# A hybrid decoder step on one core: x of three SSD groups turned to tokens by VectorE and DRAM instead of TensorE

## The chip, the core and the metric

The kernel runs on one core of a Trainium2 chip. The time is device microseconds from the first to the last instruction of an execution, with what lies around them; a few executions are taken of each kernel, and one more is recorded by the hardware profiler. Engines are named as the profile does: PE (TensorE), DVE (VectorE), ACT (ScalarE), POOL (GpSimd) and SP (SyncE), which mostly issues DMAs.

## The reference

One decoder layer is computed for 320 tokens: 256 of a prompt and 64 samples (8 sequences of 8 new tokens). `proj = rms_norm(x) @ w_in` gives the columns of a gated chunk MLP and of an SSD mixer; both results go through `w_out`, and a convolutional FFN follows. Of the mixer, the change touches the part that works on x:

```python
xbc, new_conv = causal_depthwise_conv(xbc, conv_state, conv_w, conv_b)
xbc = jax.nn.silu(xbc)
xs = xbc[..., :SSM_WIDTH].reshape(bsz, L, SSM_HEADS, SSM_HEAD_DIM)
...
xdt = (x * dt[..., None]).reshape(bsz, nc, q, G, R, P)
...
y_diag = jnp.einsum("bctsgr,bcsgrp->bctgrp", cb[..., None] * decay, xdt)
...
states = jnp.einsum("bcsgn,bcsgr,bcsgrp->bcgrpn", bc, decay_states, xdt)
```

There are 4 groups (G) of 8 heads of 64 columns. A group's x is 512 columns of `proj` by 320 tokens, and each token's x is multiplied by a step width dt per head.

## The kernel before

**Projections.** All matrix products keep the tokens in the free dimension: a weight slab of 128 x 1024 numbers is loaded by SP into `wraw` (L117), ACT rounds it to `whi` (L123), DVE takes the rest to `wlo` (L124), each with three buffers, and PE makes three products of 128 x 320 per weight block: `whi` with the high and the low part of the activations and `wlo` with the high part (L134 to L136), 24 products per slab. `project` makes columns of w_in, four blocks of 128 in four buffers of PSUM (`ps_0` to `ps_3`), `chunk_out` a part of w_out, whose sums `pd` DVE adds to `acc_mix` (L247). DVE also evacuates the projections (`ev`, L390).

**Background tasks.** Behind each slab, `tick` lets a task go one step further. `ssd(g)` is such a task, one for each group 0 to 3, called first to fourth group here. It begins with the preparation (x to tokens, xdt, cb, x0s), then `s_ps` with the products around it, and then steps n = 0 to 12 (11 in the last group), in which the states are updated, decays are made on ACT, DVE and POOL, and the outputs are multiplied. The order on each engine is that in which the program writes the instructions, but for priorities (`first`) and explicit positions (`issue_after`). `heads_in_next(g)` projects the group's x and appends the task; around the change the sequence is: heads_in of g + 1, w_out part, heads_out (z) of g. So the last steps of a group run under the w_out part, and the next group's preparation follows under its end and the start of z.

**x of a group.** `conv_proj` leaves `xs` (128 columns, 4 blocks, 320 tokens) after the last Silu (L460). At the group's start PE turns it by products with the identity: `by_token` (L412) eight times 128 x 128 for the 256 tokens of the prompt, into `xt_ps`, and DVE multiplies by dt (`times`, L925) to `xdt`. POOL multiplies the first half by a decay (`decayed`, L930, x0d), ACT and DVE split that into the parts of `x0s` (L981, L982), which `s_ps` (L991) multiplies. `x_of_samples` (L937) turns the 64 samples in four products behind `s_ps`; `samples_split` (L925, L946) and `samples_rows` (L956) multiply these. At the end of a group POOL multiplies the state `s` (L1140), and SP stores it and a second tile (L1148, L1149), to be loaded for the end of the mixer (L1160, L1161).

**B.** For the columns of B the kernel has a way without PE: `to_tokens` lets DVE turn 32 x 32 blocks (L418), for 64 tokens of four blocks at a time, POOL's queue writes them to a DRAM tile with DMAs of 32 tokens x 2 x 128 columns (L420), and loads bring rows of tokens back (L839). The 32 x 32 blocks leave the columns in an order of their own, which `in_order` undoes.

**The start.** x itself arrives in pieces by ACT's queue (`load_x`, L602): pieces of 1, 1, 2 and 2 blocks of 320 columns at first, and then two more whenever an even block has been split, six blocks ahead.

## Time and profile before

| what | us |
|---|---|
| median of 3 runs (lowest, highest) | 1748.01 (1747.86, 1748.75) |
| the profiled execution | 1748.47 |
| its span, first to last instruction | 1746.8 |
| PE busy, share of the span | 1738.5, 100% |
| DVE, ACT, POOL busy | 1178.0, 819.4, 323.5 |

Times in the trace count from the first instruction. A row of the timeline gives start, duration, engine, line, operation and operands (out<-in, shapes, count of instructions grouped), and in brackets idle time before it with what ended it. Products are pipelined: one lasts longer than the distance to the next, so PE's time is read from start to start. A "DMA to landing" row gives the least, median and greatest time from the issue of the DMAs of one line to the arrival of their data.

### The profile page before, as it was taken

Reading aid. Unit: us, or ns where it says so; the run is one execution under the profiler, and the core shown is the slowest. Engines: PE = TensorE matmul, PEld = TensorE weight load, DVE = VectorE, ACT = ScalarE, POOL = GpSimd, SP = SyncE. Lnnn points to the kernel's source line nnn. Section 1 sums busy time; section 2 is a strip of 40 time slices with the busy share of each in tenths; the row PEclk is TensorE's granted clock in tenths of the full one; section 3 lists DMA queues with packets and bytes.
Section 4 is the critical chain, followed back from the end, with each engine's and each line's share of the span. In section 5 each row is a group of like instructions: output and inputs, shape, how many; then the busy total and the mean of one; then the engine's idle time right before and its main releaser. Section 6 shows DMA issues by size and latency. Waiting matters only on the chain.

```text
span 1746.8 us, 31126 instructions
## 1 busy us (share of the span) xinstructions
PE 1738.5 (100%) x12063; PEld 1719.3 (98%) x12063; DVE 1178.0 (67%) x2009; ACT 819.4 (47%) x1198; POOL 323.5 (19%) x684
## 2 busy tenths in 40 slices
PE   9999999999999999999999999999999999999998
PEld 9999999999999999999999999999999999999997
DVE  6549863657879787778954566565756565657587
ACT  6344545334656664646544434343434343333336
POOL 2432230000423323121210101020201010101002
PEclk9999999999999999999999999999999999999999
DMA  8786655456676777665655554545544545454543
GB/s 257 230 231 183 183 176 154 151 163 192 214 221 208 218 225 210 211 187 155 195 154 151 151 154 149 150 155 147 159 145 151 155 149 152 152 153 151 148 158 109
DMA packets 228803, 303.85 MB, mean 174 GB/s; under 512 B 21680, under 2 KB 152624, under 8 KB 228464
## 3 DMA queue, kind: packets, MB, share of 16 engines
q1 hardware_dynamic: 211264, 272.68, 51.7%
q0 software_dynamic: 6176, 13.87, 2.7%
q10 hardware_dynamic: 11216, 15.31, 2.6%
q8 instruction: 95, 1.56, 0.4%
q14 instruction: 52, 0.43, 0.1%
HBM read 280.80 MB, written 19.69 MB: 172 GB/s over the span
## 4 chain that ended last, share of the span: by engine, by line
PE 99%; DMA 0%; ACT 0%; DVE 0%; SPq 0%; issue 0%; ACTq 0%
PE ps L134 21%; PE ps L135 20%; PE ps L136 20%; PE pd L134 10%; PE pd L135 10%; PE pd L136 10%; PE y_ps L1086 1%; PE ps_v L134 1%; PE ps_v L136 1%; PE ps_v L135 1%; PE yo_ps L1001 0%; PE up_ps L1018 0%; PE sg L808 0%; DMA wraw<-in_w_in 0%; PE fin_ps L1167 0%; PE xt_ps L412 0%
## 5 line engine op out<-in xcount | busy, mean ns | idle before, releaser
L124 DVE TENSOR_TENSOR wlo<-wraw,whi 128x1024 fp32r<-128x1024 f32 (+2 forms) x480 | 584.7, 1219 | 420.6 <-ACT whi L123 417.8
L123 ACT CAST whi<-wraw 128x1024 fp32r<-128x1024 f32 (+2 forms) x479 | 495.4, 1034 | 693.4 <-PE ps L135 392.3
L134 PE MATMUL ps<-h_hi,whi 128*128 128x320 f32 x2428 | 752.2, 310 | 0.0
L135 PE MATMUL ps<-h_lo,whi 128*128 128x320 f32 x2428 | 750.6, 309 | 0.0
L136 PE MATMUL ps<-h_hi,wlo 128*128 128x320 f32 x2428 | 750.0, 309 | 0.0
L134 PEld LDWEIGHTS ps<-h_hi,whi 128*128 128x128 f32 x2428 | 455.7, 188 | 3.1 <-issue 1.3
L135 PEld LDWEIGHTS ps<-h_lo,whi 128*128 128x128 f32 x2428 | 455.9, 188 | 0.4
L136 PEld LDWEIGHTS ps<-h_hi,wlo 128*128 128x128 f32 x2428 | 455.7, 188 | 0.0
L134 PE MATMUL pd<-fhi,whi 128*128 128x320 f32 x704 | 217.4, 309 | 0.0
L135 PE MATMUL pd<-flo,whi 128*128 128x320 f32 x704 | 217.4, 309 | 0.0
L136 PE MATMUL pd<-fhi,wlo 128*128 128x320 f32 x704 | 217.4, 309 | 0.0
L134 PE MATMUL pd<-ohi,whi 128*128 128x320 f32 x448 | 138.7, 310 | 0.0
L136 PE MATMUL pd<-ohi,wlo 128*128 128x320 f32 x448 | 138.3, 309 | 0.0
L135 PE MATMUL pd<-olo,whi 128*128 128x320 f32 x448 | 138.3, 309 | 0.0
L1341 POOL COPY ptf<-pad 128x2 f32<-128x2 f32 x88 | 22.0, 250 | 601.4 <-DVE pad L1329 600.8
L136 PEld LDWEIGHTS pd<-fhi,wlo 128*128 128x128 f32 x704 | 132.4, 188 | 0.0
L134 PEld LDWEIGHTS pd<-fhi,whi 128*128 128x128 f32 x704 | 132.3, 188 | 0.0
L135 PEld LDWEIGHTS pd<-flo,whi 128*128 128x128 f32 x704 | 132.3, 188 | 0.0
L247 DVE TENSOR_TENSOR acc_ffn<-acc_ffn,pd 128x320 f32<-128x320 f32 (+1 forms) x161 | 77.2, 480 | 29.8 <-PE pd L136 28.2
L134 PEld LDWEIGHTS pd<-ohi,whi 128*128 128x128 f32 x448 | 84.1, 188 | 0.6
L135 PEld LDWEIGHTS pd<-olo,whi 128*128 128x128 f32 x448 | 84.1, 188 | 0.3
L136 PEld LDWEIGHTS pd<-ohi,wlo 128*128 128x128 f32 x448 | 84.1, 188 | 0.0
(353 smaller groups left out, 1725.0 us busy)
## 6 DMA issues: line engine op xcount, KB each, us to landing
wraw<-in_ffn_w_up SPq DMA_DIRECT2D x176, 512.0 KB, 3.7
wraw<-in_w_in SPq DMA_DIRECT2D x132, 512.0 KB, 3.8
wraw<-in_ffn_w_down SPq DMA_DIRECT2D x88, 512.0 KB, 3.4
wraw<-in_w_out SPq DMA_DIRECT2D x64, 512.0 KB, 3.5
st<-in_state_ssm SPq DMA_DIRECT2D x40, 256.0 KB, 4.6
out_ssm_state_sample<-st ACTq DMA_DIRECT2D x30, 256.0 KB, 2.3
cs<-dacs_d SPq DMA_DIRECT2D x16, 320.0 KB, 5.3
wraw<-in_w_in SPq DMA_DIRECT2D x12, 384.0 KB, 3.8
```

The source lines that it names most:

```text
L123: rounded[:] = [act.copy(hi, raw).ins]
L124: lowered[:] = [dve.tensor_tensor(out=lo, in0=raw, in1=hi.bitcast(F32), op=ALU.subtract).ins]
L134: pe.matmul(ps, whi, xhi, start=first, stop=False)
L135: pe.matmul(ps, whi, xlo, start=False, stop=False)
L136: last_made[0] = pe.matmul(ps, wlo, xhi, start=False, stop=last).ins
L247: added_last[:] = [dve.tensor_tensor(out=acc[:, nb, ts], in0=acc[:, nb, ts], in1=ps[:, ts], op=ALU.add).ins]
L1086: pe.matmul(ps[64 * i:64 * i + 64, cols], w(hl), x(hl, m, cpx), tile_position=(0, 64 * i), **flags)
L1341: pool.tensor_copy(ptf[:, k, :], pad[:, 256:258])
```

## The change

For groups 1 to 3 the turning by PE goes. In steps 7, 8 and 9 of the preceding group DVE turns the 320 tokens of `xs` in five pieces of 64 (two, two, one), and POOL's queue writes each piece with two DMAs to a DRAM tile `x_d`. In step 11 two loads on POOL's queue bring the 256 prompt tokens back as `x_raw` (tag `xsp`), and at the group's start a third brings the samples as `x_raw_s`, in the tile of the tag `s1`, which `s` of the preceding group also uses. `times_raw` multiplies by dt, two instructions where there was one, for the order of the columns. `samples_rows` stands before the step, not in n == 0. The first group keeps PE's way. B's writes, which share the code, become ten DMAs of 4 x 32 x 128 in place of twenty of 32 x 2 x 128. At the start, the piece of x of blocks 4 and 5 is no longer loaded with the first, and later pieces are loaded four blocks ahead.

```diff
--- before.py
+++ after.py
@@ -356,6 +356,7 @@
     tot_d = dr.tile([NH, NB], F32, name="tot_d")
     s1_d, x1_d = ([dr.tile([P, 512], F32, name=f"{n}_d{g}") for g in range(3)] for n in ("s1", "x1"))
     b_d = dr.tile([NT, 512], F32, name="b_d")
+    x_d = [dr.tile([NT, 512], F32, name=f"x_d{g}") for g in range(1, 4)]
     v_d = [dr.tile([NT, 2 * P], F32, name=f"v_d{i}") for i in range(KD // 2)]
     ssq_d = [dr.tile([P, NT // 32], F32, name=f"ssq_d{i}") for i in range(4)]
@@ -411,13 +412,17 @@
         pe.transpose(ps, x[:, P * c:P * c + P], ident)
+    def tokens_at(x, rows, o):
+
+        t = tp.tile([P, NT], F32, tag="pv", name="turned", bufs=4)[:, :4 * NS].rearrange("p (r f) -> p r f", r=2)
+        dve.transpose(out=t.rearrange("p r (j f) -> p r j f", j=4), in_=x[:, :, o:o + NS].rearrange("p j (r t) -> p r j t", t=32))
+        for r in range(2):
+            pool.dma_start(rows[o + 32 * r:o + 32 * r + 32].rearrange("t (i f) -> i t f", i=4), t[:, r])
+
     def to_tokens(x, rows):
         for o in range(0, NT, NS):
-            t = tp.tile([P, NT], F32, tag="pv", name="turned", bufs=4)[:, :4 * NS].rearrange("p (r f) -> p r f", r=2)
-            dve.transpose(out=t.rearrange("p r (j f) -> p r j f", j=4), in_=x[:, :, o:o + NS].rearrange("p j (r t) -> p r j t", t=32))
-            for i in range(4):
-                pool.dma_start(rows[o:o + NS, P * i:P * i + P].rearrange("(r t) f -> t r f", t=32), t[32 * i:32 * i + 32])
+            tokens_at(x, rows, o)
             yield
     def in_order(ap):
@@ -601,7 +606,7 @@
                 cs = slice(KD + NT * k if k else 0, KD + NT * (k + n))
                 act.dma_start(flat[:, cs], xT[:, cs])
             with tc.high_priority(offset=300000):
-                for k, n in ((0, 1), (1, 1), (2, 2), (4, 2)):
+                for k, n in ((0, 1), (1, 1), (2, 2)):
                     load_x(k, n)
                     if k == 1:
                         act.activation(held, ones[:, 0:1], AF.Square)
@@ -616,9 +621,9 @@
                         x_split.append(act.activation(hT[0][:, kt, :], x, AF.Copy, scale=pre[:, kt:kt + 1]).ins)
                         x_low.append(dve.scalar_tensor_tensor(out=hT[1][:, kt, :], in0=x, scalar=pre[:, kt:kt + 1],
                                                               in1=hT[0][:, kt, :].bitcast(F32), op0=ALU.mult, op1=ALU.subtract).ins)
-                        if kt % 2 == 0 and kt < 10:
+                        if kt % 2 == 0 and kt < 12:
                             with tc.issue_after(x_split[-1]):
-                                load_x(kt + 6, 2)
+                                load_x(kt + 4, 2)
             def x_squares(kt):
@@ -896,7 +901,7 @@
                 return ap.rearrange("p (h d) -> p h d", d=64)
             x_of = {0: x0}
-            rest, y_made, b_later = [], {}, []
+            rest, y_made, b_later, raw_of = [], {}, [], {}
             def ssd(g):
@@ -925,6 +930,15 @@
                     dve.tensor_tensor(out=by_head(out), in0=by_head(ps),
                                       in1=dt[at, c, h0 + h.start:h0 + h.stop].unsqueeze(2).to_broadcast([at.stop - at.start, n, 64]), op=ALU.mult)
+                def times_raw(out, raw, c, at=slice(0, P), js=slice(0, 4)):
+
+                    n = raw.shape[0]
+                    for h in range(2):
+                        o = out.rearrange("p (j h i f) -> p h j i f", j=4, h=2, f=32)[:, h, js]
+                        d = dt[at, c, h0:h0 + 8].rearrange("p (j h) -> p h j", h=2)[:, h, js]
+                        dve.tensor_tensor(out=o, in0=raw[:, 256 * h:256 * h + 256].rearrange("p (i j f) -> p j i f", j=4, f=32)[:, js],
+                                          in1=d.unsqueeze(2).unsqueeze(3).to_broadcast([n, js.stop - js.start, 2, 32]), op=ALU.mult)
+
                 def decayed(i, c):
                     xde = sd.tile([P, 512], F32, tag="xde", name="xde", bufs=2)
                     pool.tensor_tensor(out=by_head(xde), in0=by_head(xdt[:, c, :]),
@@ -939,7 +953,10 @@
                 def samples_split(ps):
                     xq = sd.tile([P, 512], F32, tag="xde", name="xq", bufs=2)
-                    times(xq[:NS], ps[:NS], 3, slice(0, NS))
+                    if g:
+                        times_raw(xq[:NS], ps, 3, slice(0, NS))
+                    else:
+                        times(xq[:NS], ps[:NS], 3, slice(0, NS))
                     for i in range(2):
                         o = slice(32 * i, 32 * i + 32)
                         act.copy(xsp[o, i], xq[o])
@@ -953,16 +970,26 @@
                 def samples_rows(ps):
                     for r in range(2):
                         at, hs = slice(NS - NS * r, P - NS * r), slice(256 * r, 256 * r + 256)
+                        if g:
+                            times_raw(xdt[at, 2, :], ps, 2, slice(0, NS), slice(2 * r, 2 * r + 2))
+                            continue
                         dve.tensor_tensor(out=by_head(xdt[at, 2, hs]), in0=by_head(ps[:NS, hs]),
                                           in1=dt[:NS, 2, h0 + 4 * r:h0 + 4 * r + 4].unsqueeze(2).to_broadcast([NS, 4, 64]), op=ALU.mult)
                 for c in range(2):
-                    ps = misc("xt_ps")
-                    for j in range(4):
-                        by_token(ps[:, P * j:P * j + P], xs[:, j], c)
-                    times(xdt[:, c, :], ps, c)
+                    if g:
+                        times_raw(xdt[:, c, :], raw_of[g][0][:, c], c)
+                    else:
+                        ps = misc("xt_ps")
+                        for j in range(4):
+                            by_token(ps[:, P * j:P * j + P], xs[:, j], c)
+                        times(xdt[:, c, :], ps, c)
                     if c == 0:
                         x0d = decayed(0, 0)
+                if g:
+                    raw = sd.tile([P, 512], F32, tag="s1", name="x_raw_s", bufs=1)
+                    pool.dma_start(raw[:NS], x_d[g - 1][NP:NT])
+                    raw_of[g].append(raw)
                 ps = misc("cb_ps")
                 for c in range(2):
                     pe.matmul(ps[:, P * c:P * c + P], bT[:, g, P * c:P * c + P], cT[:, g, P * c:P * c + P],
@@ -989,7 +1016,7 @@
                 ps_s = misc("s1_ps")
                 for i, (b, x) in enumerate(((0, 0), (0, 1), (1, 0))):
                     pe.matmul(ps_s, btok[:, b, bs], x0s[:, x], start=i == 0, stop=i == 2)
-                ps_x = x_of_samples()
+                ps_x = raw_of[g][1][:NS] if g else x_of_samples()
                 ps_yo = misc("yo_ps")
@@ -1041,8 +1068,9 @@
                 for i in range(4):
                     with_c(i, sts[i] if i < 3 else st3)
                 xsp = sd.tile([P, 2, 512], F32R, tag="xsp", name="xsp", bufs=1)
+                samples_split(ps_x)
+                samples_rows(ps_x)
                 s1 = sd.tile([P, 512], F32, tag="s1", name="s1", bufs=1)
-                samples_split(ps_x)
                 act.copy(s1, ps_s)
                 strips(0)
                 yield 24, 0
@@ -1105,7 +1133,6 @@
                 decays_of = {0: (1, 2), 7 - e: (3,)}
                 for n in range(13 - e):
                     if n == 0:
-                        samples_rows(ps_x)
                         yo_to_xdt()
                     if n in ends and not (n == 10 and g == 3):
                         end(ends[n])
@@ -1125,7 +1152,15 @@
                         b_raw = sd.tile([P, 512], F32, tag="st", name="b_later", bufs=6)
                         sp.dma_start(b_raw, b_d[P:2 * P])
                         b_later.append(b_raw)
+                    if n in (7, 8, 9) and g < 3:
+                        with tc.issue_after(lowered[0]):
+                            for o in ((0, 1), (2, 3), (4,))[n - 7]:
+                                tokens_at(x_of[g + 1], x_d[g], NS * o)
                     if n == 11 and g < 3:
+                        raw = sd.tile([P, 2, 512], F32, tag="xsp", name="x_raw", bufs=1)
+                        for c in range(2):
+                            pool.dma_start(raw[:, c], x_d[g][P * c:P * c + P])
+                        raw_of[g + 1] = [raw]
                         with tc.issue_after(lowered[0]):
                             mask_c(g + 1)
                     if n in shrinks:
```

On PE, the start of the fourth group (in the order, `x8` counts instructions of one kind; `pd_13` and `pd_14` are sums of w_out, `ps_3` is the fourth block of z). Before:

```order
L136 MATMUL pd_13_7629<-ohi,wlo 128x320
L412 MATMUL xt_ps<-ident,xs 128x128 x8
L968 MATMUL cb_ps<-cT,bT 128x128 x2
L971 MATMUL cb_ps<-cT,bT 64x64 x2
...
L136 MATMUL ps_3_7713<-h_hi,wlo 128x320
L991 MATMUL s_ps<-x0s,btok 128x512 x3
L937 MATMUL xt_ps<-ident,xs 64x128 x4
L1001 MATMUL yo_ps<-st,cb_cms 32x256 x12
```

Now:

```order
L136 MATMUL pd_13_7675<-ohi,wlo 128x320
L995 MATMUL cb_ps<-cT,bT 128x128 x2
L998 MATMUL cb_ps<-cT,bT 64x64 x2
...
L136 MATMUL ps_3_7753<-h_hi,wlo 128x320
L1018 MATMUL s_ps<-x0s,btok 128x512 x3
L1028 MATMUL yo_ps<-st,cb_cms 32x256 x12
```

The eight products ahead of `cb_ps` and the four behind `s_ps` have gone; the rest of the order stays.

On POOL, from the last writes of the third group to the first work of the fourth. Before:

```order
L1140 TENSOR_TENSOR s_6732<-s_6732,dec 128x512
L1063 TENSOR_TENSOR cpx<-cpx,cT 128x256
L930 TENSOR_TENSOR xde<-xdt,dec 128x512
L1012 TENSOR_TENSOR st<-st,tote 128x512 x6
L930 TENSOR_TENSOR xde<-xdt,dec 128x512
L1063 TENSOR_TENSOR cpx<-cpx,cT 128x256
```

Now:

```order
L420 DMA x_d_108<-turned 4x32x128 x10
L1162 DMA x_raw<-x_d_108 128x512
L1175 TENSOR_TENSOR s_6763<-s_6763,dec 128x512
L1162 DMA x_raw<-x_d_108 128x512
L1091 TENSOR_TENSOR cpx<-cpx,cT 128x256
L991 DMA x_raw_s<-x_d_108 64x512
L944 TENSOR_TENSOR xde<-xdt,dec 128x512 x2
L1039 TENSOR_TENSOR st<-st,tote 128x512 x6
L1091 TENSOR_TENSOR cpx<-cpx,cT 128x256
```

Ten writes and three loads have come between, and `xde` of the fourth group, before right behind the third's last work, now stands behind the load of the samples.

On DVE, around the addition of `pd_14` and up to `x0s` of the fourth group. Before:

```order
L247 TENSOR_TENSOR acc_mix<-acc_mix,pd_13_7629 128x320
L925 TENSOR_TENSOR xdt<-xt_ps,dt 128x512
L124 TENSOR_TENSOR wlo<-wraw,whi 128x1024
L925 TENSOR_TENSOR xdt<-xt_ps,dt 128x512
L973 TENSOR_TENSOR cb_cms<-cb_ps,upper 128x256
L247 TENSOR_TENSOR acc_mix<-acc_mix,pd_14_7681 128x320
L976 TENSOR_TENSOR cb_cms<-cb_ps,upper_s 64x64
L977 TENSOR_TENSOR cb_cms<-cb_ps,upper_s 64x64
L982 TENSOR_TENSOR x0s<-xde,x0s 128x512
```

Now:

```order
L1000 TENSOR_TENSOR cb_cms<-cb_ps,upper 128x256
L124 TENSOR_TENSOR wlo<-wraw,whi 128x1024
L939 TENSOR_TENSOR xdt<-x_raw,dt 128x4x64
L247 TENSOR_TENSOR acc_mix<-acc_mix,pd_14_7721 128x320
L939 TENSOR_TENSOR xdt<-x_raw,dt 128x4x64
L1003 TENSOR_TENSOR cb_cms<-cb_ps,upper_s 64x64
L939 TENSOR_TENSOR xdt<-x_raw,dt 128x4x64 x2
L1004 TENSOR_TENSOR cb_cms<-cb_ps,upper_s 64x64
L247 TENSOR_TENSOR acc_mix<-acc_mix,pd_15_7735 128x320
L1103 TENSOR_TENSOR cs<-cs,cb_cms 128x320
L124 TENSOR_TENSOR wlo<-wraw,whi 128x1024
L1009 TENSOR_TENSOR x0s<-xde,x0s 128x512
```

The multiplications by dt are split and mixed with other work, an addition, a `cs` and a `wlo` now stand ahead of `x0s`. The turnings stand some rows earlier:

```order
L247 TENSOR_TENSOR acc_mix<-acc_mix,pd_10_7600 128x320
L418 STREAM_TRANSPOSE turned<-xs 128x256 x3
L247 TENSOR_TENSOR acc_mix<-acc_mix,pd_11_7614 128x320
L418 STREAM_TRANSPOSE turned<-xs 128x256
L124 TENSOR_TENSOR wlo<-wraw,whi 128x1024
L887 TENSOR_TENSOR cb_cms<-cmask,cT 128x128 x2
L1125 SCALAR_TENSOR_TENSOR xs<-xs,prm,y_ps 128x320
```

Three of the five are ahead of the addition of `pd_11`, the fourth behind it; the fifth follows two rows on.

## The prediction

> **What bounds the kernel now.** I read the page first: span, busy shares, granted clock, the chain that ended last.
>
> ```profile
> span 1746.8 us, 31126 instructions
> ...
> PE 1738.5 (100%) x12063; PEld 1719.3 (98%) x12063; DVE 1178.0 (67%) x2009; ACT 819.4 (47%) x1198; POOL 323.5 (19%) x684
> ...
> PEclk9999999999999999999999999999999999999999
> ```
> ```profile
> PE 99%; DMA 0%; ACT 0%; DVE 0%; SPq 0%; issue 0%; ACTq 0%
> ```
>
> PE is the chain, at full granted clock in every slice. Next, the list of what PE waited for (in all, times, longest), then the busy times of PE, PEld, DVE, ACT and POOL in the 40 us around the start of the fourth group:
>
> ```profile
> PE early L69 <- DVE ones L65: 1.1, 1, 1.1
> PE both L1454 <- ACT f_tok L1452: 1.0, 1, 1.0
> PE ps_v L134 <- ACT whi L123: 0.5, 1, 0.5
> ```
> ```profile
> 660.00:700.00 40.00, 40.00 (x314) 38.13 (x313) 29.45 (x44) 19.64 (x35) 14.78 (x11) 1.00 0.72 216
> ```
>
> Three waits, 2.6 us in all, two at the start and one in the tail: around the change PE never waits. So a matmul removed there is time saved in full, and every new wait of PE is time lost in full. The question is whether x by the new way is there as early as x by PE was.
>
> **What is removed.** PE's timeline at the start of the fourth group, where one row may hold several instructions of a kind:
>
> ```profile
> 670.01 1.03 PE L412 MATMUL xt_ps<-ident,xs 128*128 128x128 f32 x8
> 670.88 0.61 PE L968 MATMUL cb_ps<-cT,bT 128*128 128x128 f32 x4
> ```
> ```profile
> 678.86 0.85 PE L991 MATMUL s_ps<-x0s,btok 128*128 128x512 f32 x3
> 679.55 0.60 PE L937 MATMUL xt_ps<-ident,xs 128*64 128x128 f32 x4
> 680.08 1.93 PE L1001 MATMUL yo_ps<-st,cb_cms 128*32 128x256 f32 x32
> ```
>
> From start to next start the eight turnings take 670.88 − 670.01 = 0.87 us, 0.109 each. Four of the samples at that pitch are 0.44; by the start behind them 680.08 − 679.55 = 0.53, which holds a change of operand that stays. I take 0.87 + 0.44 = 1.31, at most 1.40. Three groups: **−3.92** (at most −4.2).
>
> **What DVE is given.** The five turnings per group are the operation that the trace shows for B (three in 1.09), and each multiplication of a whole x (0.69, below) becomes two halves.
>
> ```profile
> 239.14 1.09 DVE L418 STREAM_TRANSPOSE turned<-bT 128x256 f32<-128x256 f32 x3
> ```
>
> That is some 5 × 0.36 = 1.8 us, and small change for more instructions, spread over steps in which DVE is busy 29.45 of 40 us and hands wlo over before PE asks for it (PE's list of waits has no wlo). I cost it at nothing; bounds 0 and, if wlo came late by all of one step's three turnings, 1.1.
>
> **What the fourth group's x now needs.** The rows of x before: ACT's last Silu of xs, then DVE, POOL and ACT from the turned x to x0s, on which s_ps (678.86) waits:
>
> ```profile
> L460 ACT ACTIVATE xs<-cv x16: 239/243/254, 208.1 to 662.6; 128x64 f32<-128x64 f32 x16
> ```
> ```profile
> 662.97 1.23 DVE L124 TENSOR_TENSOR wlo<-wraw,whi 128x1024 fp32r<-128x1024 f32 x1
> 664.11 0.49 DVE L247 TENSOR_TENSOR acc_mix<-acc_mix,pd 128x320 f32<-128x320 f32 x1
> ```
> ```profile
> 670.65 0.69 DVE L925 TENSOR_TENSOR xdt<-xt_ps,dt 128x512 f32<-128x512 f32 x1
> ...
> 674.69 0.67 DVE L982 TENSOR_TENSOR x0s<-xde,x0s 128x512 fp32r<-128x512 f32 x1
> 675.29 0.48 DVE L1075 TENSOR_TENSOR cs<-cs,cb_cms 128x320 f32<-128x320 f32 x1
> ...
> 676.49 1.21 DVE L124 TENSOR_TENSOR wlo<-wraw,whi 128x1024 fp32r<-128x1024 f32 x1
> ```
> ```profile
> 666.44 1.88 POOL L1140 TENSOR_TENSOR s<-s,dec 128x512 f32<-128x512 f32 x1 [18.64 <-PE y_ps L1086]
> ```
> ```profile
> 671.42 1.96 POOL L930 TENSOR_TENSOR xde<-xdt,dec 128x512 f32<-128x512 f32 x1 [2.40 <-DVE xdt L925]
> ```
> ```profile
> 673.41 0.62 ACT L981 CAST x0s<-xde 128x512 fp32r<-128x512 f32 x1 [2.30 <-POOL xde L930]
> ```
>
> Before, x0s was ready at 674.69 + 0.67 = 675.4, so PE had 3.5 us to spare. Now xs is complete only at 662.6 + 0.24 = 662.9, and between it and s_ps stand DVE, ten writes and three loads on one queue. The writes are priced by B's twenty, the loads by the two loads of B (L839), the store of s ahead of the samples' load by L1148; three landing rows (min, median, max, in this order):
>
> ```profile
> 239.88 10.69 POOL L420 DMA_DIRECT2D b_d<-turned  x20 [0.91 <-DVE turned L418]
> ```
> ```profile
> DMA to landing us min/median/max: 1.8/2.8/3.8
> ```
> ```profile
> DMA to landing us min/median/max: 3.1/4.3/5.6
> ```
> ```profile
> DMA to landing us min/median/max: 2.2/2.2/2.8
> ```
>
> Step by step, with POOL in the order of the new program:
> - DVE: xs at 662.9, but behind the wlo and the addition quoted the first three turnings run from 664.5 to 664.5 + 1.09 = 665.6; the fifth needs a buffer that the first write gives back (665.8 + 2.8 = 668.6).
> - POOL issues a write in 10.69/20 = 0.53; from 665.2 on, held once by that buffer, ten end at about 670.6.
> - The load of the first 128 tokens goes out at 670.6 and lands 4.3 later, 674.9. Behind it stands POOL's s (1.88, to 673.0), then the second load: 673.0 + 4.3 = 677.3.
> - The samples' load takes the tile of s, so it waits for the store of s: 673.0 + 2.2 = 675.2, issued by 675.8. Queued behind it on POOL is x0d (1.96): 677.8; ACT's half of x0s (0.62): 678.4.
> - DVE, in its order: the second xdt at 677.3 (two halves, 0.8), a small cb and an addition (0.6), cs (0.4), wlo (1.14), x0s (0.6), where I take distances from start to start: 677.3 + 0.8 + 0.6 + 0.4 + 1.14 + 0.6 = 680.8.
>
> PE, 0.87 earlier than before, asks at 678.0: **+2.9** (680.85 − 678.0). With loads of 3.1 the second xdt starts at 676.1, but x0s stays behind ACT: 679.6, +1.6; with 5.6 it ends at 682.1, +4.1. I take the median, since both loads of B lie evenly about it. Some of it may show one step earlier, where PE needs the buffer of the addition that is behind xdt on DVE.
>
> **The other two groups.** The third group's last Silu of xs on ACT, POOL's s at the start of the second and third group, the second group's last evacuation of z on DVE, and s_ps of both:
>
> ```profile
> 565.14 0.25 ACT L460 ACTIVATE xs<-cv 128x64 f32<-128x64 f32 x1
> ```
> ```profile
> 501.31 2.03 POOL L1140 TENSOR_TENSOR s<-s,dec 128x512 f32<-128x512 f32 x1
> ```
> ```profile
> 582.33 2.03 POOL L1140 TENSOR_TENSOR s<-s,dec 128x512 f32<-128x512 f32 x1
> ```
> ```profile
> 513.73 0.48 DVE L390 TENSOR_TENSOR ev<-ps,r 128x320 f32<-128x320 f32 x1
> ```
> ```profile
> 516.82 0.85 PE L991 MATMUL s_ps<-x0s,btok 128*128 128x512 f32 x3
> ```
> ```profile
> 594.32 0.85 PE L991 MATMUL s_ps<-x0s,btok 128*128 128x512 f32 x3
> ```
>
> In the third group xs is whole at 565.4, 19 us before s is through at 584.4, and in the second the gap is longer, so the writes and the first two loads are in by then. What comes late is the samples' load. In the second group s ends at 503.3, its store lands 2.2 later, so the load is out at some 505.7 and in at 510.0. DVE's multiplications of it (1.5 in all) stand ahead of three of z's evacuations; less DVE's gaps there the last one slips by an estimated 1.1, to 514.8, and frees its buffer at 515.3. PE wants that six matmuls ahead of s_ps (1738.5/12063 = 0.144 each): 516.82 − 0.87 − 0.86 = 515.1. **+0.2**, bounds 0 and 1.0. In the third group no evacuation of z stands there; x0d (1.96), ACT (0.62) and DVE (0.67) follow s at 584.4, and x0s is ready at about 588 against 594.32: nothing.
>
> **The start.** The third piece of x now leaves the queue a step later; what PE waits for there is a weight slab:
>
> ```profile
> 8.21 0.41 PE L134 MATMUL ps_v<-h_hi,whi 128*128 128x320 f32 x1 [0.48 <-ACT whi L123]
> ```
>
> One load fewer ahead of it may bring the slab sooner by up to that 0.48 and the like before it, 0.8 in all: I take 0, bounds −0.8 and 0. B's ten writes instead of twenty free POOL for 5 us near 240, when PE waits for nothing: 0.
>
> **Sum:** −3.92 + 2.9 + 0.2 = −0.8. The profiled execution took 1748.47, 1.7 over its span and 0.46 over the median of the runs, 1748.01; the same difference on the median gives **1747.2**. The ends: −4.2 + 1.6 + 0 − 0.8 = −3.4 (1744.6) and −3.9 + 4.1 + 1.0 = +1.2 (1749.2).
>
> The Trainium skill, "DMA: Bandwidth & Descriptors", section "Why a DMA increments its semaphore by 16 and not by 1", speaks against the new writes: a DMA runs on the largest number of engines up to 16 that divides the slowest dimension of both sides. The new write has 4 there, B's old one 32, so 64 KB would go over 4 engines instead of 16. By the page's 436 GB/s over 16 engines that is an estimated 0.6 against 0.15 us per write; the stall would be 3.4 and the time 1747.7. No run here shows it yet.
>
> **Rivals.**
> - *No new wait*, −3.9, **1744.1**: turnings that start as soon as xs is there (662.9 instead of 664.5, worth 1.6) and loads of 3.1 (worth 1.3) would together take 2.9 away. For it: DVE has gaps. Against: both must hold, and DVE's list has the wlo ahead. 0.12.
> - *Loads of what was just written land late*, slower. The loads of s_d, also written shortly before, landed so:
>
> ```profile
> DMA to landing us min/median/max: 7.6/7.7/7.8
> ```
>
>  (L1161, on SP, in a burst of six.) At 7.7 instead of 4.3 the fourth group's stall grows by 3.4, and the second group's by 3.4, since there too the samples' load is what DVE stands behind: −0.8 + 6.8 = +6.0, **1754.0**. With a landing of L the sum is −0.8 + 2(L − 4.3): it turns at 4.7, and is past +3.5 from 6.45. For it: one queue, weights at 216 GB/s beside it. Against: B's loads, of the same kind on the same queue, stayed below 5.6. 0.15.
> - *The turnings are still on PE*: 1748.0. The order of the new program has no xt_ps behind the first group. 0.02.
>
> Sensitive to a rule: in the slow rival PE would stand still for 6.3 us at one place. The longest stop in PE's list is 1.1 and the clock row shows 9 throughout, so no row prices a slower clock. The Trainium skill, "TensorE: Matmul & The Clock Gate", section "What's actually happening", halves the clock after an idle window of about 3.4 us; an estimate by it is half a busy window, 1.7 us, on top of that rival, and nothing at 2.9.
>
> **How the numbers follow.** The forecast has the remaining 0.71, and its own range is 1744.6 to 1749.2. The range on record reaches down to the first rival (1744.0) and up by the 0.7 that the runs shown spread above their median (1749.9); the late loads stay outside. A measurement of this kernel tells some 0.2%, 3.5 us, from no change. Faster by that (below 1744.5): the first rival and a little of the forecast, 0.13; slower (above 1751.5): the late loads and as little, 0.16; the same: 0.71.
>
> **What would show it.** PE's rows without L412 and L937 behind the first group, cb_ps following the projection directly (−0.87 each). In PE's waits a new one of about 2.9 at the fourth group's s_ps or the step ahead of it, ended by DVE x0s or an addition; about 0.2 in the second group, none in the third. Landings of the x loads near 4.3. I am wrong if the loads land beyond 6, if POOL stands longer than 0.6 before the samples' load is out (a wait that I have mispriced), or if wlo appears in PE's waits.

## The result and the profile after

The changed kernel takes 1770.21 us in the median of 5 runs (1765.66 to 1773.57), the kernel before 1748.51 beside it: a ratio of 1.0122, with a 95% interval of 1.0111 to 1.0134. It is slower by 21.7 us, where I had forecast 0.8 us less and a range up to 1749.9. The profiled execution has a span of 1768.1, 21.3 more. First the page, then what PE waited for.

```profile
span 1768.1 us, 31157 instructions
...
PE 1744.5 (99%) x12027; PEld 1720.9 (97%) x12027; DVE 1190.0 (67%) x2039; ACT 819.9 (46%) x1198; POOL 339.0 (19%) x713
...
PEclk9999999999999998999999999999999999999999
...
PE 89%; DVE 5%; DMA 3%; ACT 1%; issue 1%; POOL 1%; SPq 0%; ACTq 0%; DVEq 0%; POOLq 0%
```
```profile
PE ps L134 <- DVE acc_mix L247: 6.8, 3, 3.2
PE ps L134 <- DVE ev L391: 5.3, 3, 3.4
PE ps L136 <- DVE wlo L124: 3.0, 2, 2.3
PE early L69 <- DVE ones L65: 1.1, 1, 1.1
PE both L1489 <- ACT f_tok L1487: 1.0, 1, 1.0
PE ps L134 <- ACT whi L123: 0.7, 1, 0.7
```

PE has 36 instructions less, and yet is busy 6 us longer; the chain is no longer PE alone. New stops of 6.8 + 5.3 + 3.0 + 0.7 = 15.8 us have come, none at s_ps, where I had looked for them first, but at ordinary products, nearly all of which wait for DVE. DVE is hardly busier (67% in both): it is late. The starts of s_ps show where; second, third and fourth group:

```profile
521.76 0.87 PE L1018 MATMUL s_ps<-x0s,btok 128*128 128x512 f32 x3
```
```profile
599.76 0.85 PE L1018 MATMUL s_ps<-x0s,btok 128*128 128x512 f32 x3
```
```profile
698.73 1.59 PE L1018 MATMUL s_ps<-x0s,btok 128*128 128x512 f32 x3
```

Before, these stood at 516.82, 594.32 and 678.86, so PE is 4.9 us late, then 5.4, then 19.9. Same products of both traces, start against start, give it finer, the gains of the removed turnings counted in: +2.0 ahead of the second group (at 488 us), +2.7 in it, +0.9 up to s_ps of the third, +7.8 behind that, +8.1 in the fourth, in all 21.5, where the span has grown by 21.3.

Three waits on DVE and POOL stand behind most of this. The fifth turning of the fourth group, with the idle time ahead of it and what ended it; then the samples' multiplication in the third, and POOL at the load for it:

```profile
686.25 0.45 DVE L418 STREAM_TRANSPOSE turned<-xs 128x256 f32<-128x256 f32 x1 [4.45 <-DMA x_d<-turned]
```
```profile
600.91 0.76 DVE L939 TENSOR_TENSOR xq<-x_raw_s,dt 64x256 f32<-64x256 f32 x2 [4.69 <-DMA x_raw_s<-x_d]
```
```profile
597.41 0.56 POOL L991 DMA_DIRECT2D x_raw_s<-x_d  x1 [4.89 <-DMA s_d<-s]
```

DVE stands 4.45 us for the buffer that the writes of the first piece must give back, and 4.69 for a load that POOL could only issue after 4.89 us, when the store of s had landed. All that is behind on DVE's queue stands too: additions that free PSUM, evacuations, wlo.

In the fourth group the wait for the buffer comes on to PE by way of the loads. The last two writes go out behind the fifth turning, the loads behind them, and DVE stands twice more for `x_raw`:

```profile
692.02 0.43 DVE L939 TENSOR_TENSOR xdt<-x_raw,dt 128x256 f32<-128x256 f32 x1 [2.63 <-DMA x_raw<-x_d]
```
```profile
694.87 1.40 DVE L939 TENSOR_TENSOR xdt<-x_raw,dt 128x256 f32<-128x256 f32 x2 [1.43 <-DMA x_raw<-x_d]
```

An addition stands right behind the first of these (692.36) and almost right behind the second (696.43), and PE's two stops there, 3.2 and 2.1 us, end with these two additions, at 692.90 and 696.96. In the third group the wait also puts DVE's work beside POOL's six multiplications of the states:

```profile
601.27 9.52 POOL L1039 TENSOR_TENSOR st<-st,tote 128x512 f32<-128x512 f32 x6 [2.24 <-PE yo_ps L1028]
```
```profile
601.70 3.37 DVE L939 TENSOR_TENSOR xdt<-x_raw_s,dt 64x128 f32<-64x128 f32 x4
604.99 2.61 DVE L1103 TENSOR_TENSOR cs<-cs,cb_cms 128x320 f32<-128x320 f32 x2
```

The four took 0.98 in the fourth group, and two such cs 0.89 in the kernel before (at 590 us), so wlo, which is next, comes some 4 us later still. In the changed kernel such a cs takes 0.48 to 0.64 in all 23 cases without a multiplication of POOL beside it, and 0.75 to 1.35 in the five that run beside one throughout; that POOL is the cause was not tried apart.

The landings, least, median and greatest, of L420 (30 writes of x, 10 of B), of the store of s (L1183) and of the samples' load (L991), and of the slabs of weights issued from 475 to 485 us, those of before and, last, those of the changed kernel:

```profile
DMA to landing us min/median/max: 2.7/5.7/7.3
```
```profile
DMA to landing us min/median/max: 2.3/3.9/5.8
```
```profile
DMA to landing us min/median/max: 2.7/3.0/3.5
```
```profile
DMA to landing us min/median/max: 4.5/5.0/5.4
```
```profile
DMA to landing us min/median/max: 7.5/7.7/7.8
```

The loads I had worried about are about as prompt as I had priced them (3.0, and 4.6 for L1162); the writes take twice my 2.8, the store of s up to 5.8 instead of 2.2, and the slabs beside the writes come 2.7 later. Ahead of the second group it is ACT that shows the effect, with an exponential that needs a load of SP (cs) and stands ahead of the next whi; before, and now:

```profile
481.44 0.42 ACT L1062 ACTIVATE cpx<-cs 128x256 f32<-128x256 f32 x1 [2.00 <-DMA cs<-dacs_d]
```
```profile
486.61 0.42 ACT L1090 ACTIVATE cpx<-cs 128x256 f32<-128x256 f32 x1 [7.23 <-DMA cs<-dacs_d]
```

ACT stands 7.23 us instead of 2.00, and whi and wlo behind it come too late for PE.

The rest is the clock. Microseconds of the fourth group, for each the busy times of PE, PEld, DVE, ACT and POOL, then the granted clock and the DMA share:

```profile
690.00:691.00 1.00, 0.00 (x0) 0.00 (x0) 0.00 (x0) 0.00 (x0) 0.98 (x3) 1.00 0.80 217
691.00:692.00 1.00, 0.00 (x0) 0.00 (x0) 0.00 (x0) 0.00 (x0) 0.58 (x1) 1.00 0.89 285
692.00:693.00 1.00, 0.10 (x1) 0.10 (x1) 0.98 (x3) 0.00 (x0) 0.00 (x0) 0.71 0.76 170
693.00:694.00 1.00, 1.00 (x4) 1.00 (x5) 0.41 (x2) 0.00 (x0) 0.00 (x0) 0.50 0.88 297
...
701.00:702.00 1.00, 1.00 (x16) 0.43 (x12) 0.99 (x4) 0.95 (x3) 0.57 (x1) 0.50 0.59 227
702.00:703.00 1.00, 1.00 (x20) 0.48 (x12) 1.00 (x2) 0.54 (x1) 1.00 (x2) 0.67 0.13 33
703.00:704.00 1.00, 1.00 (x13) 0.73 (x6) 0.98 (x1) 0.00 (x0) 1.00 (x1) 1.00 0.43 98
```

After some 3 us without products the clock is at 0.50 and stays there for 10 us. PE works in about 7.6 of these, so some 3.8 us are lost, beside the 5.3 of stops in this group (two, for additions). The same happens in the second group (518 to 522 us) and behind the third (624 to 628), some 1.6 us each. The bill: 15.8 of stops, 7.0 of clock, less 3.9 of turnings, is 18.9 of 21.3; the rest I can't assign to one cause.

### The profile page after: what moved, and what is told of

It reads as the page before. It is cut to its first block, busy times and chain, and to the rows that moved or that the text cites. A ratio compares the mean times of both kernels' runs of the same rounds, so it can differ in the third digit from the quotient of the medians.

```text
span 1768.1 us, 31157 instructions
## 1 busy us (share of the span) xinstructions
PE 1744.5 (99%) x12027; PEld 1720.9 (97%) x12027; DVE 1190.0 (67%) x2039; ACT 819.9 (46%) x1198; POOL 339.0 (19%) x713
## 4 chain that ended last, share of the span: by engine, by line
PE 89%; DVE 5%; DMA 3%; ACT 1%; issue 1%; POOL 1%; SPq 0%; ACTq 0%; DVEq 0%; POOLq 0%
PE ps L134 19%; PE ps L135 18%; PE ps L136 18%; PE pd L134 9%; PE pd L135 9%; PE pd L136 9%; DVE wlo L124 1%; PE ps_v L135 1%; PE ps_v L134 1%; PE ps_v L136 1%; DMA wraw<-in_w_in 1%; DMA x_d<-turned 1%; DVE cv L459 1%; PE yo_ps L1028 0%; DVE acc_mix L247 0%
```

## The experiments

Theories: *shape* (the new form of the writes delays them and the slabs), *samples* (their load waits for the store of s, and DVE for it), *fourth* (too little time there), *buffer* (DVE stands at the fifth turning), *traffic* (any such writes delay the slabs). The times are medians, with the ratio to the kernel before and its interval.

| run | what it is | us | ratio |
|---|---|---|---|
| e1_start_and_b | start and B's writes alone | 1748.16 | 0.9998 [0.9988, 1.0008] |
| e2_writes16 | change, old shape of writes | 1766.14 | 1.0100 [1.0084, 1.0115] |
| e3_samples_pe | change, samples by PE | 1759.26 | 1.0061 [1.0046, 1.0076] |
| e4_fourth_pe | change, fourth group by PE | 1758.30 | 1.0057 [1.0036, 1.0079] |
| e5_two_groups | the last three together | 1751.53 | 1.0019 [1.0009, 1.0028] |
| e6_turnings | before, and turnings | 1748.19 | 1.0001 [0.9991, 1.0010] |
| e7_turn_write | before, turnings, writes | 1753.88 | 1.0035 [1.0023, 1.0047] |
| e8_turn_write16 | the same, old shape | 1751.95 | 1.0021 [1.0012, 1.0031] |
| e9_four_pieces | e5 without the fifth piece | 1750.66 | 1.0013 [1.0003, 1.0022] |
| e10_writes_alone | before, writes from xs | 1748.88 | 1.0003 [0.9993, 1.0013] |
| e11_writes16_alone | the same, old shape | 1748.35 | 1.0001 [0.9992, 1.0010] |
| e12_fourth_only | fourth group by DRAM | 1755.01 | 1.0034 [1.0023, 1.0044] |
| e13_third_only | third group by DRAM | 1747.40 | 0.9996 [0.9987, 1.0004] |
| e14_second_only | second group by DRAM | 1749.85 | 1.0010 [1.0001, 1.0019] |
| e15_b_two_by_32 | B's writes 2 x 32 x 128 | 1747.99 | one run |
| e16_writes_late | e10, later source | 1749.86 | 1.0010 [1.0000, 1.0020] |
| e17_writes16_late | e11, later source | 1748.74 | 1.0003 [0.9994, 1.0012] |

### One part undone (e1 to e5)

**e1_start_and_b.** The kernel before with these lines of the change:

```diff
-                for k, n in ((0, 1), (1, 1), (2, 2), (4, 2)):
+                for k, n in ((0, 1), (1, 1), (2, 2)):
-                                load_x(kt + 6, 2)
+                                load_x(kt + 4, 2)
-                pool.dma_start(rows[o:o + NS, P * i:P * i + P].rearrange("(r t) f -> t r f", t=32), t[32 * i:32 * i + 32])
+                pool.dma_start(rows[o + 32 * r:o + 32 * r + 32].rearrange("t (i f) -> i t f", i=4), t[:, r])
```

> The kernel before with two parts of the change alone: the later load of x at the start, and B written by ten DMAs of 4 x 32 x 128 in place of twenty. x of all groups is turned by PE. Every theory that puts the loss at the groups expects the time of before, 1748.5 within 2. The rival, that the start or B's writes cost something, expects 1752 or more. In the changed kernel's trace PE stands level with before (0.1 us) up to 480 us, which speaks for the first.

1748.16: neither part costs or gains. All of the loss is at the groups.

**e2_writes16.** The change with that last line as before, for x and B.

> The changed kernel with the old shape of the writes (32 x 2 x 128, 32 KB each, twenty per group and for B). Theory 'shape': the new writes land late (median 5.7 instead of 2.8 us) because few DMA engines carry one, and slow the loads beside them; then the landing goes back to about 3, wraw's around 480 us back from 7.7 to about 5, the fifth turning no longer waits 4.45 us, and the waits of 1.96 us ahead of the second group and 1.8 ahead of the third go: about 1757 to 1763. Theory 'traffic': any such writes and loads of 1.3 MB per group delay the slabs, and the time stays at 1768 or above; POOL's longer issue (twenty of 0.54 for ten of 0.69) would add 3 to 4 us in the fourth group.

1766.14, 4 us better in the median, though the changed kernel's best run (1765.66) lies among these. PE reaches s_ps of the second group at 516.70 instead of 521.76, so shape has that place; the third and fourth lose as much as before. The time is 3 us above what I expected of shape: it is not the main cause. The wait for the buffer has not gone either, as I had expected it to: DVE stands 3.7 us for it in all, 2.3 at most.

**e3_samples_pe.**

```diff
-                ps_x = raw_of[g][1][:NS] if g else x_of_samples()
+                ps_x = x_of_samples()
```

> The changed kernel, but the 64 samples of each group are turned by PE behind s_ps as before, and the third load per group (x_raw_s) is left out; the writes stay as they are, those of the samples unused. Theory 'samples': DVE stands behind a load that waits for the store of s (landing up to 5.8 us), and the second group's 3.5 and the third's 8.2 us come from that; they go, less 0.44 us of PE per group: about 1760. If DVE's order behind the samples isn't what counts, the time stays at 1769 to 1771.

1759.26, as samples expected: the 7.8 us behind s_ps of the third group are gone, and what was lost in the second.

**e4_fourth_pe.**

```diff
-                    if n in (7, 8, 9) and g < 3:
+                    if n in (7, 8, 9) and g < 2:
```

> The changed kernel with the fourth group's x turned by PE as before (no turnings, writes and loads for it). Theory 'time is short in the fourth group': its 9.0 us of delay (less the 1.3 that PE takes again) go: 1761 to 1763. If the delay came down from the groups before it, less than 4 us go: 1766 or above.

1758.3: 11.9 us go, more than the 8 in the profile, and nothing is lost at the fourth any more. Its delay is its own. Not all of the 11.9 is: in this profile PE also loses 4.7 instead of 7.8 us behind s_ps of the third group, and the four runs lie between 1754 and 1764.

**e5_two_groups.** All three edits.

> Three causes taken away together: the old shape of the writes, the samples of every group turned by PE, and the fourth group turned by PE throughout. What is left of the change is the prompt's x of the second and third group by DRAM, eight turnings by PE less in each. If the three causes are all (and add up), the time is that of before less up to 1.7: 1746.6 to 1748.5, with perhaps 1.9 of a stop left ahead of the third group, which the changed kernel and every experiment so far show: 1748.5 to 1749. If the delay is in any turning on DVE, or in any such traffic, 1752 or more.

1751.53: 18.7 of 21.7 us go with the three, which singly gave 4.1, 11.0 and 11.9: they share some. What is left are two places where PE falls back, 1.8 at 545 us and 2.6 ahead of the third group.

### From the other end: one part added to the kernel before (e6 to e8)

```diff
                             for o in ((0, 1), (2, 3), (4,))[n - 7]:
+                                tokens_at(x_of[g + 1], x_d[g], NS * o)
```

PE turns x as before. In e6 `tokens_at` makes no writes, in e7 the new, in e8 the old ones. These kernels, and those of e10, e11, e16 and e17, also keep the start of the change and its place for `samples_rows`; e6 shows that neither costs anything.

> PE turns x of every group as before; DVE's fifteen turnings of steps 7 to 9 are made as in the changed kernel, and nothing is done with them (no writes, no loads). Theory 'DVE has no room ahead of the third group': the stop of 1.4 to 1.9 us there stays, about 1750. Theory 'DVE's turnings cost nothing' (my prediction's): 1748.4.

> As the run with the turnings alone, and POOL writes them to DRAM with the changed kernel's ten DMAs per group; nothing is loaded, PE turns x as before. Theory 'the writes over few engines delay the loads beside them': wraw's landing near 480 us rises to 7 or more, the stops of 1.96 ahead of the second and 1.8 ahead of the third group appear, and 1 to 3 more in the fourth where the fifth turning waits 4 us for a buffer and holds DVE: 1753 to 1756. Theory 'only the loads back and what waits for them cost': 1748.4 to 1750.

> The same with the old shape of the writes (twenty DMAs of 32 KB per group). Theory 'shape': the stop ahead of the second group goes, landing of the writes near 3 us, 1749 to 1751. Theory 'traffic of any shape': as the run with the new shape, within 1 us.

The turnings alone cost nothing (1748.19). With the writes it is 1753.88 or, in the old shape, 1751.95: writes that nobody reads cost up to 5.5 us. By the starts of the same products PE falls back 1.7 (new shape only), 2.6 and 1.3 us at the three groups. DVE's list of waits in e8 (in all, times, longest) names the buffer:

```profile
DVE turned L418 <- DMA x_d<-turned: 3.8, 2, 3.3
```

### Buffer or traffic (e9 to e11, e16, e17)

**e9_four_pieces**, from e5:

```diff
-                            for o in ((0, 1), (2, 3), (4,))[n - 7]:
+                            for o in ((0, 1), (2, 3), ())[n - 7]:
```

> As the run with two groups by DRAM (old shape of the writes, samples and fourth group by PE), but only the four pieces of the prompt's 256 tokens are turned and written; the piece of the samples, which nothing reads there, is left out. Theory 'buffer': DVE stands 2.6 us at the fifth turning for the buffer of the first, and this holds up additions and wlo behind it; then the stop ahead of the third group (2.6 in all) goes, and the time is 1747 to 1749. Theory 'traffic': writes beside slab loads make the stop; a fifth less of them leaves it at 2 or so: 1750.5 to 1751.5.

With four pieces for four buffers no turning waits, and the stop ahead of the third group is gone from the trace. The time, 1750.66, is only 0.9 below e5 and within what traffic expected, since the stop at 545 us stays (1.6, for wlo). By the trace buffer holds; by the time alone it would be open. A fifth buffer with all five pieces was not tried, and e9 also writes a fifth less.

**e10_writes_alone, e11_writes16_alone**, from e7 and e8:

```diff
-                                tokens_at(x_of[g + 1], x_d[g], NS * o)
+                                tokens_at(x_of[g + 1], x_d[g], NS * o, False)   # t = x[:, 0:2, 0:P]
```

> PE turns x of every group as before, nothing is turned by DVE and nothing loaded; POOL's queue makes the ten writes per group in the changed kernel's shape, in the same steps and of the same sizes, but straight from xs (so what is written is x not turned, and is not read). DVE has no buffer to wait for. Theory 'shape': the slab loads near 480 us still land late and PE stops 1.2 to 1.7 ahead of the second group, with nothing in the others: 1749.5 to 1750.5. Theory 'all of it is DVE's buffer': 1748.4. Theory 'traffic': the stops of the run with turnings and writes stay, 1752 to 1754.

> The same with twenty writes per group in the old shape. Theory 'shape' and theory 'buffer' both expect 1748.4; theory 'traffic' expects 1751 to 1752.

1748.88 and 1748.35, nothing to tell from before. But the first two blocks of xs are complete early, and the writes went out from 456 us on, in the change from 473: these two settle nothing about the second group. In e10 PE does stop 0.8 us ahead of the third, for an addition, so writes of the new shape can cost something there without any turning. **e16_writes_late, e17_writes16_late** take `x[:, 3, 0:2 * P]`, the block that comes last:

> PE turns every group's x, no turnings, no loads; the ten writes per group in the changed kernel's shape take the last block of xs as their source and so fall into the steps in which the changed kernel writes. Theory 'writes beside slab loads': stops ahead of the second and third group as in the run with turnings and writes (1.7 and 2.6): 1751 to 1753. Theory 'coupling to DVE' (both are needed, the later slab and DVE's own work or its wait for a buffer): at most 0.6 in all, 1748.0 to 1749.0.

> The same with twenty writes in the old shape. Theory 'writes beside slab loads': 1750 to 1752. Theory 'coupling to DVE': 1748.0 to 1748.7.

In the old shape still nothing (1748.74). In the new shape PE falls back 1.5 us ahead of the second group, and nowhere else (1749.86). The same row of ACT, in e16 and in e17:

```profile
485.34 0.42 ACT L1080 ACTIVATE cpx<-cs 128x256 f32<-128x256 f32 x1 [6.79 <-DMA cs<-dacs_d]
```
```profile
483.27 0.42 ACT L1080 ACTIVATE cpx<-cs 128x256 f32<-128x256 f32 x1 [4.33 <-DMA cs<-dacs_d]
```

and SP's issue of the slab beside it (start, duration):

```profile
480.24 1.60 SPq L117 DMA_DIRECT2D wraw<-in_w_in  x1
```
```profile
477.99 0.39 SPq L117 DMA_DIRECT2D wraw<-in_w_in  x1
```

Beside writes of the new shape SP takes 1.60 us for an issue that takes 0.39 beside the old, and 1.01 instead of 0.46 for the load of cs ahead of it; the slab goes out 2.2 us later. It is no single case: four issues in a row at this place take 0.60 to 1.17 in the changed kernel and 0.53 to 1.74 in e7, but 0.40 to 0.52 in e8, with the old shape. The slabs themselves land late in both (7.1 and 7.5): traffic delays them, but it is the later issue that passes what is in hand. So at that place the shape alone does it; of the stops of the third and fourth group these two runs show none above 0.3 us, and e7 and e8, where DVE turns and then waits, show them.

**e15_b_two_by_32**, whether shape or size:

```diff
-            for i in range(4):
-                pool.dma_start(rows[o:o + NS, P * i:P * i + P].rearrange("(r t) f -> t r f", t=32), t[32 * i:32 * i + 32])
+            for r in range(2):
+                for i in range(2):
+                    pool.dma_start(rows[o + 32 * r:o + 32 * r + 32, 256 * i:256 * i + 256].rearrange("t (i f) -> i t f", i=2), t[64 * i:64 * i + 64, r])
```

> The kernel before, with B's twenty writes of 32 KB in the form 2 x 32 x 128 instead of 32 x 2 x 128, nothing else. Theory 'shape': they land later than the 1.8/2.8/3.8 us of before, at 4 us or more in the median, as the ten of 4 x 32 x 128 do (2.7/4.6/6.2 there). Theory 'size': 2.8 to 3.0. The time of the run is 1748 to 1749 in both, since no one waits there.

The writes in e15, their issue and landing:

```profile
L421 POOL DMA_DIRECT2D b_d<-turned x20: 661/661/754, 239.4 to 252.4; - x20
...
DMA to landing us min/median/max: 2.7/4.9/6.2
```

At the same 32 KB and the same count a slowest dimension of 2 instead of 32 takes the median from 2.8 to 4.9 and POOL's issue from 0.54 to 0.66. Bytes, count and place are the same, so it is the shape, in one profiled execution of each.

### One group alone (e12 to e14)

From e9, with the group in the two conditions:

```diff
-                    if n in (7, 8, 9) and g < 2:
+                    if n in (7, 8, 9) and (g == 2):
```

(`g == 2` for the fourth group, 1 for the third, 0 for the second.)

> Only the fourth group's x of the prompt goes by DRAM (four pieces, sixteen writes in the old shape), all samples and the other groups are turned by PE. Theory 'time is short there', with the loads at 4 to 5 us: xs is complete at 663, sixteen writes take POOL 16 x 0.54 = 8.6 us, so the loads go out at about 674 and land at 678 to 681: PE stops 3 to 6 us at s_ps or the step ahead of it, gains 0.87, and the clock falls behind a stop of that length: 1752 to 1756. Theory 'the fourth inherits its delay from the groups before': 1747.5 to 1748.5.

> Only the third group's x of the prompt goes by DRAM, everything else by PE. If eight turnings less are worth their 0.87 us where nothing new is waited for: 1747.2 to 1747.5 (0.05% faster, at the edge of what five rounds tell). If the writes and loads make a stop by themselves: 1749 or more.

> Only the second group's x of the prompt goes by DRAM, everything else by PE. If the 1.8 us left at 545 us belong to the second group (its later norm on DVE): 1749 to 1750, the stop of 1.6 at wlo in PE's waits. If they come from both groups together: 1747.2 to 1748.5.

The fourth alone: 1755.01, 6.7 slower. PE's one new stop is at s_ps, where the prediction had it, and the clock falls with it:

```profile
PE s_ps L1008 <- ACT x0s L998: 3.5, 1, 3.5
```
```profile
682.00:683.00 1.00, 0.00 (x0) 0.00 (x0) 1.00 (x3) 0.40 (x1) 0.00 (x0) 0.62 0.00 0
683.00:684.00 1.00, 0.73 (x2) 0.49 (x3) 1.00 (x2) 0.22 (x1) 0.00 (x0) 0.50 0.00 0
...
688.00:689.00 1.00, 1.00 (x12) 0.44 (x12) 0.35 (x1) 0.98 (x2) 0.10 (x1) 0.50 0.00 0
689.00:690.00 1.00, 1.00 (x15) 0.38 (x8) 0.97 (x2) 0.84 (x2) 0.99 (x1) 0.97 0.13 33
```

A stop of 3.5 costs some 3 more: PE works nearly six microseconds at half clock. The runs say the same: of the eight, six took 1754.9 to 1755.6 us at a mean granted clock of 0.997, and two took 1751.7 and 1751.8 at 0.999. So the clock costs about 3.3 us where it falls, and it does not fall each time. The third alone is 1747.40, with no new stop, its s_ps at

```profile
592.62 0.86 PE L1008 MATMUL s_ps<-x0s,btok 128*128 128x512 f32 x3
```

and the span at 1745.4. PE is 0.9 ahead of where it was at the group's start, as the eight turnings say; the time can't be told from before. The second alone is 1749.85: the 1.8 us at 545 us are its own, where PE waits for DVE's olo of the first group's norm. DVE is late there because it stands longer for a load of that norm, in the kernel before and in e14:

```profile
532.13 0.23 DVE L320 TENSOR_REDUCE small<-small 128x10 f32<-128x40 f32 x1 [1.39 <-DMA small<-ssq_d]
```
```profile
534.32 0.23 DVE L320 TENSOR_REDUCE small<-small 128x10 f32<-128x40 f32 x1 [4.21 <-DMA small<-ssq_d]
```
```profile
528.11 0.33 SPq L1175 DMA_DIRECT2D x_d<-xde  x1
528.66 1.30 SPq L319 DMA_DIRECT2D small<-ssq_d  x3
```

SP issues these loads at 528.66 instead of 526.89, behind the store of the group's second tile, which it makes at 528.11 instead of 516.62. That tile, the second `xde`, is now multiplied by POOL behind its six `st` (at 527.04 instead of 509.89). The same order stands in the traces of e3, e5 and e9, which also leave the samples on PE, but not in that of the changed kernel, which loses nothing at 545 us. It is not all of it: e2 and e4, without this order, lose 0.6 and 1.0 us there. No run puts the order back.

## Why the prediction was wrong, step by step

The step that failed by most: I followed each new wait mainly along the path of x to x0s, and priced the waits by writes and stores that land early. DVE makes its instructions in the program's order, so what it waits for holds additions, evacuations and wlo too, none of which needs x, and PE stopped for these: in the third group behind the wait of 4.69 us, in the fourth behind the loads that the wait of 4.45 us had put off. Term by term:

- **What is removed, 0.87 per group: right.** e13 gains 0.9 at the start of its group. The samples' 0.44 shows too: in the changed kernel PE's lag falls from 5.4 to 5.0 behind s_ps of the third group.
- **The start and B, 0: right** (e1).
- **DVE's turnings, 0: right alone** (e6), wrong in company. I had DVE "held once by that buffer" for the fifth turning and counted the delay for POOL's writes only. Held is the whole queue of DVE: 4.45 us in the fourth group, since the first four writes there land 6.0 to 6.6 after their issue, not 2.8, and 1.42 in the third, where PE falls back 1.7 us ahead of s_ps. Without the fifth piece that place loses nothing (e9). The bound that I set, a wlo late by "all of one step's three turnings", was for another wait.
- **Writes land in 2.8: the first step that failed.** I priced a write of 4 x 32 x 128 by rows of 32 x 2 x 128. It takes 0.69 to issue, where I had 0.53, and 5.7 to land, and SP's loads beside it go out and land later. The Trainium skill, "DMA: Bandwidth & Descriptors", section "Why a DMA increments its semaphore by 16 and not by 1", names this (few engines for a small slowest dimension). I worked from its bandwidth an estimate of 0.45 us, and e15 shows 2.1 in the median (for 2 x 32 x 128; the form itself, in B's writes of e1, 1.8, from 2.8 to 4.6). The records do not name the engine of a packet, so that few engines carry a write is the rule's account; the effect of the shape is measured.
- **The samples' load, +0.2 in the second and nothing in the third group: one of the two dearest steps (e3 takes 11.0 us away, e4 11.9).** I took 2.2 for the store of s, the row of a quiet SP queue, and asked only whether x0s and the evacuations were in time. In the third group I left out that the multiplications of the samples stand on DVE ahead of cs and wlo: DVE stood 4.69 us and worked slowly behind it, gave no slab buffer back, and SP issued no slab from 595.7 to 608.8 us.
- **Fourth group, +2.9: right in kind, wrong in size.** Alone it is 3.5 (e12); with the wait for the buffer and the late writes 5.3 in two stops, for the additions behind xdt on DVE, as "one step earlier" said. The loads' own landing was priced well (3.7 and 4.6, I had 4.3); what came before them was late.
- **The clock, "nothing at 2.9": wrong.** I let a rule stand outside the sum because no row priced it. A stop of 3.5 brought the clock to 0.50 for nearly 7 us (e12), and in the second group a stretch with PE busy 0.34, 0.41, 0.74 and 0.60 of four microseconds, its longest single stop 1.2, was enough. The Trainium skill, "TensorE: Matmul & The Clock Gate", section "What's actually happening", states half the clock after an idle window of some 3.4 us; the trace agrees on the half, but the window need not be all idle. Nor does such a stretch always bring the clock down: in e4 stops of 1.4, 0.7 and 0.4 at the same place left it at 1.00. In the changed kernel it falls at 518.34, 624.15 and 692.42 us, 31 and 20 times 3.413 us apart; as I read it, where a stop lies on this grid decides too.
- **The rival that ended slower** had the loads of x late (7.7). They landed at 4.6 (L1162), so it did not come true, though the time was slower still. Late were the writes and the store of s. That DVE stands behind the samples' load it had right, for the second group alone.
- **The sum.** I added terms, each with its own slack, and they don't add: turnings alone stop PE nowhere (e6), writes of the old shape alone cost at most 0.4 us (e17), together they cost 3.6 (e8). One reason is measured, the wait for the buffer, which needs both. That all draw on one slack besides, the slabs that are loaded ahead, is my reading and not shown apart.

## What to carry to other kernels

Before pricing a wait of an in-order engine, list what else is behind it and which buffers that work gives back: a wait of DVE that nobody needed cost PE more here than the work it replaced. Price a DMA by rows of the same shape, not only the same size. And price a stop of a PE that has never stood still at up to twice its length, until a trace says otherwise.

## What was not expected of the hardware

The shape of a DMA's access changes what it costs the issuing engine (POOL 0.54, 0.66 and 0.69 us for 32 x 2 x 128, 2 x 32 x 128 and 4 x 32 x 128, the last with twice the bytes) and others: one issue on SP took 1.60 us beside writes of the new shape (e16) and 0.39 beside those of the old (e17). For each 64 tokens four DMAs of the old shape instead of two of the new gave the lower median in all three pairs (e2, e8, e17), by 4.1, 1.9 and 1.1 us; the runs of each pair overlap a little.
